# Silu gates by a hyperbolic tangent out of PSUM, and reciprocal square roots wholly on the vector engine, in the last two layers of a four-layer kernel

## The chip, the cores and the metric

The kernel runs on one core of a Trainium2 chip. The metric is the device time of one launch in microseconds (us), the median of several runs. The engines are named as in the profile: PE is the matrix engine (PEld its weight loads, which overlap it), DVE the vector engine, ACT the scalar engine, POOL the GpSimd engine, and SP the engine that issues most of the transfers.

## The reference, cut to what matters

Four layers work on 512 tokens of width 1024 in fp32. The change is in the last two: a differential attention and a neighbourhood attention, both over 512 tokens and a context of 256, both with an inner width of 2048, which the kernel splits into eight groups g.

```python
def diff_attention_mixer(u_lat, u_ctx, w_in, w_out, qn_g, kn_g, lam_vecs, subln_g, layer_idx, need_ctx):
    ...
        return (o.reshape(bsz, n, D_INNER) * jax.nn.silu(z)) @ w_out
...
def neighbourhood_mixer(u_lat, u_ctx, w_in, w_out, qn_g, kn_g, rpb, need_ctx):
    ...
    out_l = (o_l * jax.nn.silu(z_l)) @ w_out
...
def rms_norm(x, g):
```

In both, q and k are divided per head (64 wide) by their root mean square, the scores go through a softmax, and the output o of a head is multiplied by silu(z) = z / (1 + exp(-z)), where z is a projection of the layer's input. In the differential layer two softmaxes are subtracted, and o is divided by its own root mean square over 128 columns before the gate. So each layer needs, for every group, one set of gates and a few reciprocal square roots of small tiles (128 x 24, 128 x 16 or 128 x 6).

## The kernel before, in words

Each of the two layers is one loop over units that is written out by hand: in the differential layer (`diff_run`) a unit is (g, p, t), 12 to a group, 96 in all; in the neighbourhood layer (`na_run`) it is (g, h, j), 16 to a group, 128 in all. In every iteration the stages of neighbouring units stand in a fixed order in program text, and each engine takes its own instructions in that order: the scores of the new unit on PE (A), work that was put off by one iteration (`due`, which runs what `defer` took), one projection piece for the next group on PE, the minimum of the negated scores on DVE (B, L2116 and L2286), the transposes of the unit before on PE (T, L2152 and L2304), the exponentials on ACT (E), a second projection piece in some iterations, the value product on PE (G), and the scaling of the exponentials on DVE (Dm, L2138 to L2140 and L2296 to L2297). T of the next iteration waits for Dm. With t0 the first unit of a group, "t0+3" below is the fourth iteration of a group.

The projection pieces are 24 matmuls of 128x256 (a "mm" buffer in PSUM each) whose weights come as `w_raw` by SP, are rounded to `w_hi` by ACT (CAST, L276) and split into `w_lo` by POOL (L280). A piece of q or k leaves PSUM by ACT as `st` (a copy) and `sq` (its square), and DVE sums the square per head into `ssq` or `ssk` (L1777). When the last sum of a group is there, `finish` makes the reciprocal root by `rstd_parts`: L422 on DVE, a logarithm and an exponential on ACT, and one iteration later three operations of a Newton step on DVE (L432 to L434) and up to two scalings (L1792, L1795). `Hn` does the same for the 128 x 6 tile `oss` of a finished pair of heads, with its Newton step at L2180 to L2183; POOL then multiplies the output `ob` by the result (L2184). `H2` transposes `ob`, and DVE multiplies it by the gate (L2194).

A piece of z leaves PSUM by an ACT copy into `SZ`. `gates_at` sets out for every 128 columns of it an ACT exponential into `ge`, and an iteration later on DVE an addition (L1829) and a RECIPROCAL (L1830), and on POOL the product with z (L1831). In the neighbourhood layer the gate multiplies the output in POOL (L2331).

Of the kernel before, what the change touches and what calls it, by code (L numbers as in the profile page):

```python
# [380 lines left out]
class Net:  # L381
# [1254 lines left out]
    def tables2(s, pool, tmp):  # L1636
# [11 lines left out]
        def compute():  # L1648
# [26 lines left out]
    def second(s, L, nx):  # L1675
# [108 lines left out]
        def finish(n, g, k):  # L1784
            r = g2.tile([128, 24], F32, name=f"r{n}")
            rs = s.rstd_parts(r[:, :k], SS[n][:, :k], 1.0 / 64)
            next(rs)

            def two():
                next(rs, None)  # L1790
                if n == "q":
                    nc.vector.tensor_scalar(r[:, :k], r[:, :k], 0.125, None, OP.mult)  # L1792
                    if diff:
                        r2 = g2.tile([128, 24], F32, name="nrq")
                        nc.vector.tensor_scalar(r2, r, -1.0, None, OP.mult)  # L1795
                        scal[g] = r, r2
                        return
                for i in range(k // 4):
                    x = rawt[n][:, i].rearrange("p (h d) -> p h d", d=64)
                    nc.gpsimd.tensor_tensor(x, x, r[:, 4 * i:4 * i + 4].unsqueeze(2).to_broadcast([128, 4, 64]), OP.mult)  # L1800

            s.defer(two)

        def z_piece(g, b, t0):
            box = {}

            def mm():
                if t0 == 0:
                    hold("z", [f"z{L}:{g}:{b}"])
                box["ps"] = ps = s.mm.tile([128, 512], F32, name="mm")[:, :256]  # L1810
                for h in range(2):
                    s.fmm(ps, U["z"], uh, ul, t0, 256, ks=range(4 * h, 4 * h + 4))
                    yield

            return mm, lambda: s.act(SZ[g][b][:, t0:t0 + 256], box["ps"], AF.Copy)

        def gates_at(ts, g, chunks):

            e = {}

            def one(b, c):
                z = SZ[g][b][:, c * 128:(c + 1) * 128]
                e[b, c] = g2.tile([128, 128], F32, name="ge", bufs=3 if diff else 4)
                s.act(e[b, c], z, AF.Exp, scale=-1.0)

            def two(b, c):
                z = SZ[g][b][:, c * 128:(c + 1) * 128]
                x = e[b, c]
                nc.vector.tensor_scalar(x, x, 1.0, None, OP.add)  # L1829
                nc.vector.reciprocal(x, x)  # L1830
                nc.gpsimd.tensor_tensor(z, z, x, OP.mult)  # L1831

            for t, bc in sorted([(t + 1, (0, bc)) for t, bc in zip(ts, chunks)] + [(t, (1, bc)) for t, bc in zip(ts, chunks)]):
                put((early, extra)[bc[0]], t, lambda bc=bc: (two, one)[bc[0]](*bc[1]))

# [63 lines left out]
        def put(d, t, *x):  # L1899
            d.setdefault(t, []).extend(x)  # L1900

        ns = 12 if diff else 16
        for g in range(8):
# [3 lines left out]
            if diff and g < 7:  # L1907
# [4 lines left out]
                for j in range(6):  # L1912
                    put(fill, t0 + j, *qk[2 * j:2 * j + 2])
                at = (6, 6, 7, 8, 8, 9, 9, 10, 11, 12, 13, 14) if g < 6 else (6, 7, 7, 8, 8, 9, 13, 13, 14, 14, 15, 15)
                gates_at([t0 + t for t in at], g, [(b, c) for b in range(2) for c in range(6)])
                for t, f in zip((6, 7, 8, 9), stacks("q", 0) + stacks("k", 0)):
# [5 lines left out]
            elif diff:  # L1922
                for t, x in zip(Z7, zz):
                    put(fill, t0 + t, x)
                put(extra, t0 + 2, lambda: y_tile(), *[lambda b=b: y_dma(b) for b in range(5)])
                gates_at([t0 + t for t in (4, 5, 6, 7, 8, 9, 10, 11, 12, 13, 14, 15)], g, [(b, c) for b in range(2) for c in range(6)])
                put(extra, t0 + 5, lambda: y_dma(5))
                for b in range(8):
                    put(early, t0 + Y7[b], lambda b=b: y_split(b))
            else:  # L1930
                if g < 7:
                    vv = [piece("v", g + 1, i) for i in range(6)]
                    for t, x in zip((0, 1, 2, 3, 4, 5, 6, 7, 8, 9, 10, 11, 12, 13) + ((13, 14, 14, 15, 15, 16) if g < 6 else (14, 15, 15, 16, 16, 17)), qk + zz + vv):
# [143 lines left out]
    def diff_run(s, c):  # L2077
# [93 lines left out]
        def Hn(g, p):  # L2171
            o, ss, oe = O[g, p]
            v, y, a = [s.sml.tile([128, 6], F32, name=f"df_{k}") for k in "vya"]
# [12 lines left out]
            s.defer(two)  # L2186
# [45 lines left out]
    def na_run(s, c):  # L2232
# [158 lines left out]
```

## Time and profile before

| | |
|---|---|
| median of three runs | 3164.03 us (3159.46 to 3167.75) |
| profiled execution | 3165.68 us, span 3163.9 us, mean granted clock 0.990 |
| busy: PE, DVE, ACT, POOL | 3051.2, 1903.7, 1611.1, 1739.4 us |
| loop of the differential layer | about 1450 to 2260 us of the span, some 100 us a group |
| loop of the neighbourhood layer | about 2435 to 3060 us, some 83 us a group |

The times inside the kernel come from the profiled execution, whose time is 1.65 us over the median. PE is busy for 96 parts in a hundred of the span, so a change shows in the time where it makes PE wait, or stops a wait of PE.

### The profile page before, as it was taken

To read this page: it belongs to the slowest core of one execution; us is meant where nothing else is said; L and a number is where in the kernel's file an instruction comes from. 1 tells how busy PE (TensorE), PEld (TensorE's weight loads), DVE (VectorE), ACT (ScalarE), POOL (GpSimd) and SP (SyncE) were. 2 spreads that over 40 slices of the span, in tenths; PEclk is the share of its full clock that TensorE was granted. 3 is DMA by queue.
4 is the path that set the end of the run, shared out by engine and by line. 5 is a ranking of instruction groups with operands and counts; after the bars stand their busy time and mean duration, and the time that the engine had idled before them with its cause. 6 is when DMAs were issued, how large, how long until landed. Compare 5 with 4: busy or idle time off the path is not lost.

```text
span 3163.9 us, 59874 instructions
## 1 busy us (share of the span) xinstructions
PE 3051.2 (96%) x22868; PEld 2878.0 (91%) x22868; DVE 1903.7 (60%) x4163; ACT 1611.1 (51%) x3811; POOL 1739.4 (55%) x2390
## 2 busy tenths in 40 slices
PE   8999999998999999999999999998999999999989
PEld 7898889888899988899999999998999999999989
DVE  4875423345775333355777777677445777777764
ACT  4544533345775433345655555555325565656652
POOL 5543466664663656667556665563356545555545
PEclk9999999999999999999999999999999999999989
DMA  3122333434233434442222222213323233333334
GB/s 124 61 74 82 106 127 127 143 115 149 94 92 116 136 125 133 129 125 78 69 71 65 71 70 69 69 57 107 124 94 94 73 85 88 85 91 91 88 94 141
DMA packets 104555, 310.89 MB, mean 98 GB/s; under 512 B 19902, under 2 KB 33470, under 8 KB 100684
## 3 DMA queue, kind: packets, MB, share of 16 engines
q1 hardware_dynamic: 94908, 271.60, 26.3%
q0 software_dynamic: 7776, 31.46, 4.3%
q10 hardware_dynamic: 1584, 4.00, 0.4%
q8 instruction: 181, 2.97, 0.4%
q14 instruction: 106, 0.87, 0.1%
HBM read 258.73 MB, written 23.12 MB: 89 GB/s over the span
## 4 chain that ended last, share of the span: by engine, by line
PE 63%; DVE 4%; ACT 3%; DMA 2%; POOL 2%; issue 1%; SPq 0%; ACTq 0%; DVEq 0%; POOLq 0%
PE mm L587 16%; PE mm L589 16%; PE mm L588 16%; PE mm L2165 3%; PE tp L2304 2%; PE s L2105 1%; PE tp L2152 1%; DMA KL<-KL 1%; PE s L2106 1%; PE mm L2319 1%; PE mm L2314 1%; PE tp L1843 1%; PE s L2278 1%; ACT X L413 1%; POOL w_lo L280 1%
## 5 line engine op out<-in xcount | busy, mean ns | idle before, releaser
L280 POOL TENSOR_TENSOR w_lo<-w_raw,w_hi 128x256 fp32r<-128x256 f32 (+2 forms) x1438 | 1142.4, 826 | 804.2 <-ACT w_hi L276 771.1
L587 PE MATMUL mm<-w_hi,hh 128*128 128x256 f32 (+2 forms) x2752 | 801.9, 291 | 9.9 <-ACT w_hi L276 4.4
L588 PE MATMUL mm<-w_lo,hh 128*128 128x256 f32 (+2 forms) x2752 | 784.5, 285 | 5.8 <-POOL w_lo L280 3.9
L589 PE MATMUL mm<-w_hi,hl 128*128 128x256 f32 (+2 forms) x2752 | 783.5, 285 | 1.5 <-POOL hl L416 1.5
L587 PEld LDWEIGHTS mm<-w_hi,hh 128*128 128x128 f32 x2752 | 525.1, 191 | 20.0 <-ACT df_sq L413 6.3
L588 PEld LDWEIGHTS mm<-w_lo,hh 128*128 128x128 f32 x2752 | 525.7, 191 | 15.2 <-POOL w_lo L280 9.8
L589 PEld LDWEIGHTS mm<-w_hi,hl 128*128 128x128 f32 x2752 | 524.4, 191 | 3.0 <-POOL hl L416 2.2
L276 ACT CAST w_hi<-w_raw 128x1024 fp32r<-128x1024 f32 (+2 forms) x371 | 383.3, 1036 | 227.8 <-PE mm L589 186.2
L587 PE MATMUL mm<-hh,w_hi 128*128 128x256 f32 (+1 forms) x1408 | 454.8, 323 | 3.0 <-DVE M L1092 2.8
L588 PE MATMUL mm<-hl,w_hi 128*128 128x256 f32 (+1 forms) x1408 | 447.8, 318 | 0.6
L589 PE MATMUL mm<-hh,w_lo 128*128 128x256 f32 (+1 forms) x1408 | 446.5, 317 | 0.6 <-DVE w_lo L280 0.6
L587 PEld LDWEIGHTS mm<-hh,w_hi 128*128 128x128 f32 x1408 | 265.5, 189 | 30.9 <-issue 5.2
L587 PE MATMUL mm<-w_hi,gh 128*128 128x256 f32 x1024 | 287.8, 281 | 0.0
L589 PE MATMUL mm<-w_hi,gl 128*128 128x256 f32 x1024 | 287.2, 280 | 0.1
L588 PE MATMUL mm<-w_lo,gh 128*128 128x256 f32 x1024 | 287.0, 280 | 0.0
L588 PEld LDWEIGHTS mm<-hl,w_hi 128*128 128x128 f32 x1408 | 265.5, 189 | 22.3 <-DVE hl L347 1.8
L589 PEld LDWEIGHTS mm<-hh,w_lo 128*128 128x128 f32 x1408 | 265.1, 188 | 21.4 <-DVE w_lo L280 1.0
L416 DVE TENSOR_TENSOR gl<-rsq,gh 128x512 fp32r<-128x512 f32 x64 | 46.0, 719 | 269.1 <-ACT gh L413 269.1
L587 PEld LDWEIGHTS mm<-w_hi,gh 128*128 128x128 f32 x1024 | 193.2, 189 | 0.4
L589 PEld LDWEIGHTS mm<-w_hi,gl 128*128 128x128 f32 x1024 | 193.0, 188 | 0.5 <-DVE gl L416 0.5
L588 PEld LDWEIGHTS mm<-w_lo,gh 128*128 128x128 f32 x1024 | 193.0, 188 | 0.3
L413 ACT ACTIVATE wt<-tp 128x512 f32<-128x512 f32 (+1 forms) x96 | 50.5, 526 | 229.9 <-PE tp L2152 229.9
(385 smaller groups left out, 6963.5 us busy)
## 6 DMA issues: line engine op xcount, KB each, us to landing
w_raw<-in_w SPq DMA_DIRECT2D x352, 512.0 KB, 3.5
modw<-in_mod SPq DMA_DIRECT2D x24, 1024.0 KB, 5.9
KH<-KH POOLq DMA_DIRECT2D x32, 384.0 KB, 3.6
KL<-KL POOLq DMA_DIRECT2D x32, 384.0 KB, 4.9
xs<-X SPq DMA_DIRECT2D x12, 512.0 KB, 3.8
X<-xs SPq DMA_DIRECT2D x12, 512.0 KB, 7.1
yd<-ob SPq DMA_DIRECT2D x16, 384.0 KB, 2.4
w_raw<-in_w SPq DMA_DIRECT2D x8, 552.0 KB, 3.6
```

Of the source, the lines that this page charges most:

```text
L276: nc.scalar.copy(hi[:, :m], raw[:, :m])
L280: (eng or nc.gpsimd).tensor_tensor(lo[:, c], raw[:, c], hi.bitcast(F32)[:, c], OP.subtract)
L413: return s.nc.scalar.activation(out, in_, func, bias=bias, scale=scale, **kw)
L416: (eng or s.nc.vector).tensor_tensor(lo, x, hi.bitcast(F32), OP.subtract)
L587: mm(ps, ah, bh, start=first, stop=False)
L588: mm(ps, ah, bl, start=False, stop=False)
L589: mm(ps, al, bh, start=False, stop=last)
L1843: nc.tensor.transpose(pt[:, j], rawt[n][:, i, pr * 128:(pr + 1) * 128], s.ident)
L2105: nc.tensor.matmul(o, q, KH[:, h, a:b], start=True, stop=False)
L2106: nc.tensor.matmul(o, q, KL[:, h, a:b], start=False, stop=True)
L2165: nc.tensor.matmul(ps, x["w"][:, k], V[g][:, kb, p * 128:(p + 1) * 128], start=k == 0, stop=k == nk - 1)
L2304: nc.tensor.transpose(t[:, k], x["P"][:, k * 128:(k + 1) * 128], s.ident)
```

## The change

The gate is written as silu(z) = z/2 * (1 + tanh(z/2)). ACT reads the z piece in PSUM and writes tanh(z/2) for all 256 columns into `ge`, and one DVE operation, SCALAR_TENSOR_TENSOR, makes (ge + 1) * z out of `ge` and the same PSUM buffer straight into `SZ`; it runs at once in the differential layer and one iteration later in the neighbourhood layer. The factor of one half goes into `gs` and into the scaling of P in Dm. `gates_at` and its calls go. The reciprocal roots of these two layers are made by `rstd_root`: a guess of the square root from the bits of the number, two steps of Heron's rule, and a last reciprocal, 9 or 10 operations of DVE in one piece, at once in `finish`; in `Hn` 11 operations, all put off to the next iteration's `due`. No logarithm is left in the two layers, and the set of ACT's tables is changed by hand at their start and at the end of the first.

```diff
+    def rstd_root(s, r, ss, inv_n, c, eps=EPS):
+
+        n = r.shape[-1]
+        v = s.nc.vector
+        q, a = [s.small.tile([128, 24], F32, name=f"rr_{k}")[:, :n] for k in "qa"]
+        v.tensor_scalar(ss, ss, inv_n, eps, OP.mult, OP.add)
+        v.tensor_scalar(q.bitcast(I32), ss.bitcast(I32), 0.5, float(0x1FBB4F2E), OP.mult, OP.add)
+        v.reciprocal(a, q)
+        v.tensor_tensor(a, a, ss, OP.mult)
+        v.tensor_tensor(q, q, a, OP.add)
+        v.reciprocal(a, q)
+        v.tensor_tensor(a, a, ss, OP.mult)
+        v.scalar_tensor_tensor(q, q, 0.25, a, OP.mult, OP.add)
+        v.reciprocal(r, q)
+        if c != 1.0:
+            v.tensor_scalar(r, r, c, None, OP.mult)
...
-            nc.vector.tensor_scalar(gs, s.p("subln"), 1.0 - lam_init, None, OP.mult)
+            nc.vector.tensor_scalar(gs, s.p("subln"), 0.5 * (1.0 - lam_init), None, OP.mult)
...
-            r = g2.tile([128, 24], F32, name=f"r{n}")
-            rs = s.rstd_parts(r[:, :k], SS[n][:, :k], 1.0 / 64)
-            next(rs)
+            r = g2.tile([128, 24], F32, name=f"r{n}")[:, :k]
+            s.rstd_root(r, SS[n][:, :k], 1.0 / 64, 1.0 if n == "k" else -0.125 if diff else 0.125)
...
-            return mm, lambda: s.act(SZ[g][b][:, t0:t0 + 256], box["ps"], AF.Copy)
-
-        def gates_at(ts, g, chunks):
...
-                e[b, c] = g2.tile([128, 128], F32, name="ge", bufs=3 if diff else 4)
-                s.act(e[b, c], z, AF.Exp, scale=-1.0)
...
-                nc.vector.tensor_scalar(x, x, 1.0, None, OP.add)
-                nc.vector.reciprocal(x, x)
-                nc.gpsimd.tensor_tensor(z, z, x, OP.mult)
...
+            def ev():
+
+                ps, e = box["ps"], g2.tile([128, 256], F32, name="ge")
+                s.act(e, ps, AF.Tanh, scale=0.5)
+                mult = lambda: nc.vector.scalar_tensor_tensor(SZ[g][b][:, t0:t0 + 256], e, 1.0, ps, OP.add, OP.mult)
+                mult() if diff else s.defer(mult)
...
+        nc.scalar.preload_act_table_set(TANHEXP)
...
+        if diff:
+            nc.scalar.preload_act_table_set(LNEXP)
...
-            nc.vector.scalar_tensor_tensor(oe, oe, EPS, oe, OP.mult, OP.mult)
-            nc.vector.scalar_tensor_tensor(v, ss, 1.0 / 128, oe, OP.mult, OP.add)
-            s.act(y, v, AF.Ln)
-            s.act(y, y, AF.Exp, scale=-0.5)
+            y = s.sml.tile([128, 6], F32, name="df_y")
...
-                nc.vector.tensor_tensor(a, y, y, OP.mult)
-                nc.vector.tensor_tensor(a, a, v, OP.mult)
-                nc.vector.tensor_scalar(a, a, -0.5, 1.5, OP.mult, OP.add)
-                nc.vector.tensor_tensor(y, y, a, OP.mult)
+                nc.vector.scalar_tensor_tensor(oe, oe, 128 * EPS, oe, OP.mult, OP.mult)
+                nc.vector.tensor_tensor(ss, ss, oe, OP.add)
+                s.rstd_root(y, ss, 1.0 / 128, 1.0, 0.0)
...
-            nc.vector.tensor_scalar(x["P"], x["P"], r, None, OP.mult)
+            nc.vector.tensor_scalar(x["P"], x["P"], r, 0.5, OP.mult, OP.mult)
```

The order of instructions on DVE in a differential group, at t0+3 of `diff_run`, from Dm of one iteration to B of the next. Before:

```order
L2140 SCALAR_TENSOR_TENSOR X_66<-X_67,df_rb,X_66 128x768
L2174 SCALAR_TENSOR_TENSOR oe<-oe 128x6
L2175 SCALAR_TENSOR_TENSOR df_v<-oss,oe 128x6
L1777 TENSOR_REDUCE ssq<-sq 128x4 x2
L422 TENSOR_SCALAR rs_v<-ssq 128x24
L2180 TENSOR_TENSOR df_a<-df_y 128x6
L2181 TENSOR_TENSOR df_a<-df_a,df_v 128x6
L2182 TENSOR_SCALAR df_a<-df_a 128x6
L2183 TENSOR_TENSOR df_y<-df_y,df_a 128x6
L2116 ISA s_18167,df_nb<-s_18167,zero,nrq 128x768
```

After, where L446 to L456 are the lines of `rstd_root` and L2114 is B:

```order
L2138 SCALAR_TENSOR_TENSOR X_66<-X_67,df_rb,X_66 128x768
L1795 TENSOR_REDUCE ssq<-sq 128x4 x2
L446 TENSOR_SCALAR ssq<-ssq 128x24
L447 TENSOR_SCALAR rr_q<-ssq 128x24
L448 RECIPROCAL rr_a<-rr_q 128x24
...
L456 TENSOR_SCALAR rq<-rq 128x24
L2174 SCALAR_TENSOR_TENSOR oe<-oe 128x6
L2175 TENSOR_TENSOR oss<-oss,oe 128x6
L446 TENSOR_SCALAR oss<-oss 128x6
...
L454 RECIPROCAL df_y<-rr_q 128x6
L2114 ISA s_18124,df_nb<-s_18124,zero,rq 128x768
```

Between the last sum of squares and B there stood five operations; now there are the ten of the root for q and the eleven of `Hn`.

The same engine in a neighbourhood group, at t0+10 of `na_run`, where the last sum of squares of k comes. Before:

```order
L1777 TENSOR_REDUCE ssk<-X_69 128x4
L422 TENSOR_SCALAR rs_v<-ssk 128x24
L2286 ISA s_29822,na_nb<-s_29822,bm_29265 128x512
L2286 ISA na_nb 128x1
L416 TENSOR_TENSOR ptl<-tp,pth 128x512
L2296 RECIPROCAL na_r<-na_s 128x1
L2297 TENSOR_SCALAR X_66<-X_66,na_r 128x512
L432 TENSOR_TENSOR rs_a<-rs_y 128x24
```

After, where L2279 is B and L2290 the scaling in Dm:

```order
L1795 TENSOR_REDUCE ssk<-X_69 128x4
L446 TENSOR_SCALAR ssk<-ssk 128x24
L447 TENSOR_SCALAR rr_q<-ssk 128x24
L448 RECIPROCAL rr_a<-rr_q 128x24
L449 TENSOR_TENSOR rr_a<-rr_a,ssk 128x24
...
L454 RECIPROCAL rk<-rr_q 128x24
L2279 ISA s_29511,na_nb<-s_29511,bm_28952 128x512
L2279 ISA na_nb 128x1
L417 TENSOR_TENSOR ptl<-tp,pth 128x512
L2289 RECIPROCAL na_r<-na_s 128x1
L2290 TENSOR_SCALAR X_66<-X_66,na_r 128x512
```

One operation stood ahead of B there, and now nine do.

Later in the same group, at t0+13, where gates were made. Before:

```order
L2286 ISA s_30122,na_nb<-s_30122,bm_29266 128x512
L416 TENSOR_TENSOR ptl<-tp,pth 128x512
L1829 TENSOR_SCALAR ge<-ge 128x128
L1830 RECIPROCAL ge<-ge 128x128
...
L2296 RECIPROCAL na_r<-na_s 128x1
L2297 TENSOR_SCALAR X_66<-X_66,na_r 128x512
```

After:

```order
L1831 SCALAR_TENSOR_TENSOR SZ<-ge,mm 128x256
...
L2279 ISA s_29811,na_nb<-s_29811,bm_28953 128x512
L2279 ISA na_nb 128x1
L417 TENSOR_TENSOR ptl<-tp,pth 128x512
L2289 RECIPROCAL na_r<-na_s 128x1
L2290 TENSOR_SCALAR X_66<-X_66,na_r 128x512
```

The two pairs L1829 and L1830 ahead of Dm are gone there, and the new operation of the gate stands ahead of an earlier B.

## Rows read from the trace of the kernel before

**Rows 1.** The page, part 1: busy time, share of the span, instructions.
```profile
PE 3051.2 (96%) x22868; PEld 2878.0 (91%) x22868; DVE 1903.7 (60%) x4163; ACT 1611.1 (51%) x3811; POOL 1739.4 (55%) x2390
```
**Rows 2.** A window of 100 us: busy of PE, PEld, DVE, ACT, POOL; clock; DMA.
```profile
1750.00:1850.00 100.00, 98.30 (x808) 96.13 (x808) 73.72 (x170) 57.15 (x173) 60.61 (x92) 1.00 0.23 69
```
**Rows 3.** Waits of PE, 1450 to 2100 us: total, times, longest.
```profile
PE tp L1843 <- DVE ob L2194: 8.5, 6, 1.4
...
PE mm L587 <- ACT df_sq L413: 0.9, 6, 0.2
```
**Rows 4.** Waits of PE, 2100 to 2290 us.
```profile
PE s L2105 <- ACT X L413: 5.1, 6, 1.4
PE tp L2152 <- DVE X L2140: 5.0, 2, 4.7
```
**Rows 5.** Waits of PE, 2460 to 3000 us.
```profile
PE tp L2304 <- DVE X L2297: 7.3, 12, 2.0
PE s L2278 <- DMA KL<-KL: 2.1, 6, 0.7
```
**Rows 6.** Waits of PE, 3000 to 3164 us.
```profile
PE tp L2304 <- DVE X L2297: 5.3, 3, 4.4
PE s L2277 <- DMA KH<-KH: 2.3, 1, 2.3
```
**Rows 7.** A window at the last group change, same columns.
```profile
2990.00:3020.00 30.00, 24.39 (x175) 23.55 (x175) 20.98 (x46) 14.44 (x39) 10.14 (x19) 0.89 0.33 88
```
**Rows 8.** Groups of instructions: count, busy us, mean ns, idle before.
```profile
L1830 DVE RECIPROCAL ge<-ge 128x128 f32<-128x128 f32 x160 | 152.5, 953 | 5.5
...
L413 ACT ACTIVATE X<-s,na_nb 128x512 f32<-128x512 f32 x128 | 87.7, 685 | 30.5 <-DVE na_nb L2286 30.1
...
L2296 DVE RECIPROCAL na_r<-na_s 128x1 f32<-128x1 f32 x128 | 18.4, 144 | 3.9 <-ACT X L413 3.8
```
**Rows 9.** Timeline of DVE at 1579, ahead of B.
```profile
1578.64 0.42 DVE L1777 TENSOR_REDUCE ssq<-sq 128x4 f32<-128x256 f32 x1 [0.43 <-ACT sq L413]
...
1579.18 0.16 DVE L2180 TENSOR_TENSOR df_a<-df_y 128x6 f32<-128x6 f32 x1
1579.38 0.17 DVE L2181 TENSOR_TENSOR df_a<-df_a,df_v 128x6 f32<-128x6 f32 x1
...
1579.86 1.02 DVE L2116 CUSTOM_DVE_ANT_0 s<-s,zero,nrq 128x768 f32<-128x768 f32 x1
```
**Rows 10.** Timeline of ACT at 1583 to 1587.
```profile
1583.21 0.92 ACT L413 ACTIVATE X<-s,df_nb 128x768 f32<-128x768 f32 x1
...
1584.96 1.07 ACT L276 CAST w_hi<-w_raw 128x1024 fp32r<-128x1024 f32 x1
1586.58 0.28 ACT L413 ACTIVATE ob<-mm 128x128 f32<-128x128 f32 x1 [0.55 <-PE mm L2165]
```
**Rows 11.** Timeline of PE at 1587.
```profile
1587.16 0.39 PE L587 MATMUL mm<-w_hi,hh 128*128 128x256 f32 x1
```
**Rows 12.** Timeline of DVE at 2561 to 2563: B and the scaling in Dm.
```profile
2561.40 0.69 DVE L2286 CUSTOM_DVE_ANT_0 s<-s,bm 128x512 f32<-128x512 f32 x1
...
2563.26 0.49 DVE L2297 TENSOR_SCALAR X<-X,na_r 128x512 f32<-128x512 f32 x1
```
**Rows 13.** Timeline of PE at 2564.7: the transposes of T.
```profile
2564.70 0.60 PE L2304 MATMUL tp<-ident,X 128*128 128x128 f32 x4
```
**Rows 14.** Timeline of ACT at 54: a load of tables and the next operation.
```profile
54.23 1.28 ACT L413 ACT_TABLE_LOAD   x1
55.52 0.21 ACT L413 ACTIVATE cg<-par 128x16 f32<-128x16 f32 x1
```
**Rows 15.** Timeline of all engines at 1586, two rows of POOL and DVE.
```profile
1585.89 1.37 POOL L1773 TENSOR_TENSOR st<-X,X 128x256 f32<-128x256 f32 x1
...
1586.58 0.73 DVE L432 TENSOR_TENSOR rs_a<-rs_y 128x24 f32<-128x24 f32 x1
```
**Rows 16.** Waits of PE, 1389 to 1450 us: the differential layer's start.
```profile
PE mm L587 <- ACT sq L413: 1.8, 1, 1.8
```

More of the change, by code (lines that the diff above doesn't have):

```diff
@@ L30 @@
 LNEXP = "natural_log_exp_and_others"
+TANHEXP = "exp_and_others"
 def plan():
@@ L1784, in finish @@
         def finish(n, g, k):
-            r = g2.tile([128, 24], F32, name=f"r{n}")
-            rs = s.rstd_parts(r[:, :k], SS[n][:, :k], 1.0 / 64)
-            next(rs)
+            r = g2.tile([128, 24], F32, name=f"r{n}")[:, :k]
+            s.rstd_root(r, SS[n][:, :k], 1.0 / 64, 1.0 if n == "k" else -0.125 if diff else 0.125)
             def two():
[L1790 to L1797, printed above, removed]
+                if n == "q" and diff:
+                    scal[g] = r
+                    return
                 for i in range(k // 4):
@@ L1813, in mm @@
                     yield
-            return mm, lambda: s.act(SZ[g][b][:, t0:t0 + 256], box["ps"], AF.Copy)
-        def gates_at(ts, g, chunks):
-            e = {}
-            def one(b, c):
-                z = SZ[g][b][:, c * 128:(c + 1) * 128]
-                e[b, c] = g2.tile([128, 128], F32, name="ge", bufs=3 if diff else 4)
-                s.act(e[b, c], z, AF.Exp, scale=-1.0)
-            def two(b, c):
-                z = SZ[g][b][:, c * 128:(c + 1) * 128]
-                x = e[b, c]
-                nc.vector.tensor_scalar(x, x, 1.0, None, OP.add)
-                nc.vector.reciprocal(x, x)
-                nc.gpsimd.tensor_tensor(z, z, x, OP.mult)
-            for t, bc in sorted([(t + 1, (0, bc)) for t, bc in zip(ts, chunks)] + [(t, (1, bc)) for t, bc in zip(ts, chunks)]):
-                put((early, extra)[bc[0]], t, lambda bc=bc: (two, one)[bc[0]](*bc[1]))
+            def ev():
[3 more added lines that the diff above has]
+                mult() if diff else s.defer(mult)
+            return mm, ev
         def stack(n, pr, tiles):
@@ L1913, in second @@
                     put(fill, t0 + j, *qk[2 * j:2 * j + 2])
-                at = (6, 6, 7, 8, 8, 9, 9, 10, 11, 12, 13, 14) if g < 6 else (6, 7, 7, 8, 8, 9, 13, 13, 14, 14, 15, 15)
-                gates_at([t0 + t for t in at], g, [(b, c) for b in range(2) for c in range(6)])
                 for t, f in zip((6, 7, 8, 9), stacks("q", 0) + stacks("k", 0)):
@@ L1925, in second @@
                 put(extra, t0 + 2, lambda: y_tile(), *[lambda b=b: y_dma(b) for b in range(5)])
-                gates_at([t0 + t for t in (4, 5, 6, 7, 8, 9, 10, 11, 12, 13, 14, 15)], g, [(b, c) for b in range(2) for c in range(6)])
                 put(extra, t0 + 5, lambda: y_dma(5))
@@ L1934, in second @@
                         put(fill, t0 + t, x)
-                    gates_at([t0 + t for t in (12, 13, 13, 14, 14, 15, 15, 16)], g, [(b, c) for b in range(2) for c in range(4)])
                     for t, f in zip((12, 13, 14), stacks("q", 0) + stacks("k", 0)):
@@ L1945, in second @@
                         put(fill, t0 + t, x)
-                    gates_at([t0 + t for t in (7, 8, 9, 10, 11, 12, 13, 14)], g, [(b, c) for b in range(2) for c in range(4)])
                     put(extra, t0 + 2, *[lambda b=b: y_dma(b) for b in range(6)])
@@ L2110, in B @@
             x = d[u]
-            nrq = c.scal[g][1]
+            nrq = c.scal[g]
             for j in range(2):
@@ L2172, in Hn @@
             o, ss, oe = O[g, p]
-            v, y, a = [s.sml.tile([128, 6], F32, name=f"df_{k}") for k in "vya"]
-            nc.vector.scalar_tensor_tensor(oe, oe, EPS, oe, OP.mult, OP.mult)
-            nc.vector.scalar_tensor_tensor(v, ss, 1.0 / 128, oe, OP.mult, OP.add)
-            s.act(y, v, AF.Ln)
-            s.act(y, y, AF.Exp, scale=-0.5)
+            y = s.sml.tile([128, 6], F32, name="df_y")
             def two():
-                nc.vector.tensor_tensor(a, y, y, OP.mult)
-                nc.vector.tensor_tensor(a, a, v, OP.mult)
-                nc.vector.tensor_scalar(a, a, -0.5, 1.5, OP.mult, OP.add)
-                nc.vector.tensor_tensor(y, y, a, OP.mult)
+                nc.vector.scalar_tensor_tensor(oe, oe, 128 * EPS, oe, OP.mult, OP.mult)
+                nc.vector.tensor_tensor(ss, ss, oe, OP.add)
+                s.rstd_root(y, ss, 1.0 / 128, 1.0, 0.0)
                 nc.gpsimd.tensor_tensor(o, o, y.unsqueeze(2).to_broadcast([128, 6, 128]), OP.mult)
```

## The prediction

> **What bounds the kernel now.** I read the busy shares first: PE is busy 3051.2 of 3163.9 us [rows 1], so no other engine's work is worth its length; only waits of PE count, and those are 3163.9 - 3051.2 = 112.7 us in the whole kernel, most of them outside these two layers. Second, the windows: in 100 us of the differential loop PE is busy 98.30, at full clock, with DVE at 73.72, ACT at 57.15 and POOL at 60.61 [rows 2]. Third, the waits of PE, stage by stage. In the differential loop the only wait that repeats with weight is that of the transposes of q and k pieces for the gate's product `ob`, 8.5 us over 6 groups [rows 3]; that product follows the transposes of `H2`, which stand behind a Dm, not behind a gate. In the tail of that loop PE waits 5.1 us for the exponentials and 5.0 for Dm [rows 4]. In the neighbourhood loop it waits 7.3 us at T for Dm, in 12 pieces, the longest 2.0, and 2.1 us for the transfer of KL [rows 5]; in the last group 5.3 us at T and 2.3 for KH [rows 6]. Around the last group change the granted clock is 0.89 [rows 7], a part of the window at the lower of the two levels, after PE had idled.
>
> **What the change removes.** On DVE 160 reciprocals of 953 ns go, 152.5 us [rows 8], with the additions ahead of them; on POOL the 160 products; on ACT two small operations for each root and 160 exponentials, while the tanh takes the place of the copy out of PSUM. In the differential loop that is nearly all work beside a busy PE and worth nothing by itself. It is worth something where a gate stands ahead of what PE waits for:
>
> The neighbourhood loop, at t0+12 to t0+15. In the order before, one or two gates stand between `ptl` and Dm; the reciprocal alone is 0.95 us [rows 8]. After, none do. So I take the waits at T there as gone, without the longest: 7.3 - 2.0 = 5.3, and the waits for KL with them, 2.1, since POOL and ACT reach that transfer earlier: a gain of 7.4 us. Bounds: 3 (T's alone, in part) and 9.4 (all of it).
>
> The last group change and the last group, 2.0 + 5.3 = 7.3 us of waits at T. Here a transfer of KH is right behind (2.3 us) [rows 6], whose wait grows when PE comes to it earlier, so I take 3 of 7.3. Bounds: 0 and 7.3, and above that what the clock gives back: at 0.89 of 30 us [rows 7] that is 3.3 us.
>
> The tail of the differential loop: of 10.1 us [rows 4] most is ACT's own pace and I take 2. Bounds: 0 and 10.1.
>
> Gains together: 7.4 + 3 + 2 = 12.4 us.
>
> **What it adds.** *The price of a chain.* Small operations of DVE start 0.20 us apart [rows 9]. A reciprocal takes 144 ns on one column and 953 on 128 [rows 8], 6.4 ns a column, so I estimate 0.29 us on 24 columns and 0.18 on 6, with 0.04 between. The root of q has 7 other operations and 3 reciprocals: 7 x 0.20 + 3 x 0.33 = 2.4 us; that of k has one operation less, 2.2; that of `Hn` 8 x 0.20 + 3 x 0.22 = 2.3.
>
> *Differential loop, t0+3.* The sums end at 1578.64 + 0.42 = 1579.06 and B starts at 1579.86 [rows 9]. With both chains ahead of it (the first two order listings) B starts at 1579.06 + 2.4 + 2.3 = 1583.8, that is 3.9 us later. The first exponential started at 1583.21 [rows 10], though B's first minimum was there at 1579.86 + 1.02 = 1580.9; so 2.3 us are slack and the exponentials come 1.6 late. Queued behind them on ACT is the rounding of weights, which ended at 1584.96 + 1.07 = 1586.03, and then the copy of the value product, `ob`, at 1586.58: slack again 0.55, so this copy is 1.05 us late. The first matmul of the next piece, at 1587.16 [rows 11], takes that buffer and waits for it already (for `df_sq`) [rows 3]. A loss of 1.05 us in each of 7 groups: 7.4 us. Bounds: at operations of 0.16 us, their bare length [rows 9], the two slacks hide it, 0; if POOL stands in the way, below.
>
> *Differential loop, t0+6 and t0+8.* At t0+6 the chain of k, 2.2 us, takes the place of one operation ahead of B; a slack of 2.3 like the one at t0+3 hides it, and at t0+8 the eleven operations of `Hn` replace four and a turn through ACT. I take 0; without that cover the first costs up to 2.0 in 6 groups, 12 us.
>
> *Neighbourhood loop, t0+10.* Nine operations instead of one ahead of B (the third and fourth order listings): B comes 2.2 - 0.2 = 2.0 us later than at 2561.40 [rows 12]. The exponential waits for nothing but B (30.1 of 30.5 us of its idle time) [rows 8], so Dm ends at 2563.26 + 0.49 + 2.0 = 2565.75. T started at 2564.70 [rows 13], so PE waits 1.05 us; in 7 groups 7.4 us. Bounds: 0.5 a group at bare lengths (3.5), 2 if the slack is gone. The chain of q, five iterations before, has a value product ahead of the next T and I take it as covered.
>
> *The tables.* A load of ACT's tables takes 1.28 us, and the next operation starts 1.29 after it did [rows 14]. Three are added. The one at the differential layer's start stands ahead of the pieces' first copies, where PE waits for ACT already (1.8 us) [rows 16]; so does that at the next layer's start; the third is followed by transfers and I take it as hidden: 2 x 1.3 = 2.6 us. Bounds: 0 and 3.9. The Trainium skill, "ScalarE: Activation LUTs", section "What ACT_TABLE_LOAD costs", puts a change of tables at about 2.66 us, a load of 1283 ns and a drain of some 1380. The load agrees with the row; no drain shows there, and by the page's figure the two would be 5.3 us, 2.7 more than in the sum.
>
> *The gate's own operation.* 80 of them, in place of two reciprocals each; behind Dm in the differential layer and one iteration late in the other; nothing is due behind them that PE waits for. 0.
>
> **The sum.** 7.4 + 7.4 + 2.6 - 12.4 = +5.0 us on the profiled 3165.7, so 3170.7; the median is 1.65 lower, so 3169 us. That is 0.16% over before: no change that this measurement can tell (0.3%, 9.5 us).
>
> **The rivals.**
> *The chains are hidden, and what went pays* (faster). Both losses rest on slacks read in one group each, 2.3 and 0.95 us, while ACT and DVE lose work ahead of these places. If half a microsecond more of slack stands at each, the losses fall to about 7, and if all of it is hidden there remain 2.6 - 12.4 = -9.8, with the clock 3.3 more: 3151 to 3156. It decides from chains under 2.7 us for both at t0+3 (less than 0.13 an operation) or E's turn coming later anyway. Against it: the order of B is fixed behind the chains.
>
> *The chains meet POOL* (slower). The Newton operation at 1586.58 took 0.73 us and ended with a POOL operation that had begun at 1585.89 and lasted 1.37 [rows 15], where others take 0.16 [rows 9]. If the 6 or 7 operations of a chain that are not reciprocals each take 0.5 longer, a chain of q or k costs 3 us more; if half of the 14 chains in the two loops are hit, 7 x 3 = 21 us: 3190. For it: POOL is busy 60 of 100 us [rows 2]. Against it: at t0+3 and t0+10 the operations around B ran at 0.16 to 0.20, and POOL waits there for the chain's own result. The Trainium skill, "SBUF — State Buffer", section "Who interferes with whom", says the same as a rule: an operation of DVE with two inputs in SBUF, or one in a mode with two ports, waits out an operation of GpSimd that reads SBUF. The row agrees; by this rule the four operations of each root with two tensors are the exposed ones.
>
> *The loads of tables and the last transfers.* If nothing is gained at the last group change (KH is waited for instead) and the tables cost 5, the time is 3175: just over the bound.
>
> **How the numbers follow.** The forecast has 0.52; its own range is 3160 to 3178, of which 0.38 lies within 0.3%, 0.12 above and 0.02 below. The first rival has 0.27 (0.25 faster, 0.02 same), the second and third 0.21, slower. So faster 0.27, same 0.40, slower 0.33. The range reaches into both rivals: down to 3148 (most of the hidden chains with the clock), up to 3190 (half of the chains hit).
>
> **What would show it.** In the waits of PE of the changed kernel: T's waits in the neighbourhood loop no longer at t0+13 and t0+14 but one a group at t0+10, of about 1 us; a wait of the first matmul of a piece for `df_sq` of about 1.3 us a group in place of 0.15; the rows of `ob` as before. In DVE's timeline at t0+3: 21 operations over 4.7 us, reciprocals at 0.29 and 0.18. Three table loads of 1.28 us. The prediction is wrong if the chains take under 3 us or over 7 at t0+3, if exponentials of the differential layer are not queued ahead of the copy of `ob`, or if the clock's dips come or go elsewhere.

## The result

The changed kernel takes 3183.59 us (median of five runs, 3181.22 to 3187.63) against 3160.77 of before in the same five rounds (3159.46 to 3167.75): a ratio of 1.0067, 95% interval 1.0056 to 1.0077. It is slower by some 21 us. The forecast was 3169, no change, with 0.33 for slower; the time lies inside the range of 3148 to 3190, on the slow side of it.

The page of the changed kernel, part 1, as in [rows 1]:

```profile
PE 3051.1 (96%) x22868; PEld 2877.3 (90%) x22868; DVE 1785.8 (56%) x4155; ACT 1568.6 (49%) x3558; POOL 1651.9 (52%) x2230
```

PE does the same work in the same 22868 matmuls, while DVE does 118 us less, ACT 43 and POOL 87. The kernel is slower all the same. The profiled execution took 3181.51 us, 15.8 more than the profiled one of before, whose 3165.68 was 4.9 above its own median of five; so the traces show 15.8 of the 21 us, and the rest is the spread of single executions. A part of that spread is the clock's: the profiled execution of before was granted 0.990, while 34 of the 44 executions of before beside the experiments were granted 0.991 or 0.992, and 0.001 of the clock is up to 3.2 us of such a span. The profiled execution of the changed kernel was granted 0.990 too, so the 15.8 us as a whole are not the clock's, though single stages are in part, as said below.

Since PE runs the same matmuls in the same order in every kernel of this study but for its waits, the k-th matmul of one trace can be set against the k-th of another: the difference of their starts says how far a kernel is behind, and the growth of that difference says where it fell behind. The table gives this growth by stages of before's time, in us, and the last column the whole of it. Every entry is two starts from PE's timelines, subtracted.

| kernel | to 1390 | first start, to 1480 | differential loop, to 2110 | its tail, to 2400 | second start, to 2470 | neighbourhood loop, to 2990 | rest | all |
|---|---|---|---|---|---|---|---|---|
| changed | 1.7 | 3.3 | 9.6 | -0.5 | 3.8 | 1.9 | -4.1 | 15.9 |
| e1_roots | 1.9 | -0.4 | 8.4 | 3.5 | 2.8 | 8.8 | -0.1 | 24.9 |
| e2_noroot | 2.4 | 3.3 | 0.1 | -1.8 | -2.6 | -6.5 | -4.3 | -9.3 |
| e3_late | 0.8 | 5.1 | 7.7 | -1.0 | 4.2 | 3.8 | -5.4 | 15.2 |
| e4_tab | 1.1 | -0.3 | 9.8 | -1.2 | 4.6 | 2.3 | -3.2 | 13.2 |
| e5_start | 0.2 | -0.5 | 9.9 | -1.8 | -1.3 | 2.3 | -4.6 | 4.1 |
| e6_place | 1.3 | 5.1 | 0.3 | -0.3 | 2.5 | -6.8 | -4.0 | -2.0 |
| e7_all | 1.3 | -0.4 | 0.3 | -3.0 | 0.6 | -6.2 | -4.2 | -11.6 |
| e8_hn | 5.2 | 1.3 | 34.0 | 3.4 | 0.5 | 2.2 | -2.7 | 44.1 |
| e9_dose | 2.6 | 3.3 | 24.0 | 1.8 | 4.2 | 2.0 | -3.5 | 34.5 |
| e10_block | 0.2 | 4.7 | 9.5 | 4.8 | 4.0 | 2.1 | -3.9 | 21.4 |

Nothing was changed before 1390 us, so the first column, 0.2 to 5.2, is how far two executions differ by themselves; it is the measure for what a single entry can say.

**The profile after.** Waits of PE from 1450 to 2100 us (total, times, longest), against [rows 3]:

```profile
PE tp L1843 <- DVE ob L2187: 8.5, 6, 1.4
PE mm L605 <- ACT df_sq L414: 6.9, 12, 1.1
PE mm L2163 <- DVE SZ L1831: 1.9, 6, 0.4
```

The wait for `ob` is the same 8.5 us to the tenth. That for `df_sq` went from 0.9 to 6.9, and one for the gate's new operation (SZ, 1.9) is new. DVE's timeline at t0+3, against [rows 9]: the last sum, the first operation of q's root and a reciprocal of it, a reciprocal of the pair's root, and B.

```profile
1584.48 0.42 DVE L1795 TENSOR_REDUCE ssq<-sq 128x4 f32<-128x256 f32 x1 [0.78 <-ACT sq L414]
1584.93 0.18 DVE L446 TENSOR_SCALAR ssq<-ssq 128x24 f32<-128x24 f32 x1
...
1585.36 0.30 DVE L448 RECIPROCAL rr_a<-rr_q 128x24 f32<-128x24 f32 x1
...
1588.13 0.19 DVE L448 RECIPROCAL rr_a<-rr_q 128x6 f32<-128x6 f32 x1
...
1589.49 0.99 DVE L2114 CUSTOM_DVE_ANT_0 s<-s,zero,rq 128x768 f32<-128x768 f32 x1
```

Twenty-one operations take 1589.49 - 1584.93 = 4.6 us. The first matmul of the next piece, the one of [rows 11], in PE's timeline:

```profile
1593.93 0.38 PE L605 MATMUL mm<-w_hi,hh 128*128 128x256 f32 x1 [1.12 <-ACT df_sq L414]
```

It waits 1.12 us for the release by `df_sq`. Set against its time in the trace of before it fell back by 0.97 us at this instruction.

The neighbourhood loop, against [rows 5]:

```profile
PE tp L2297 <- DVE X L2290: 8.8, 13, 1.1
PE s L2271 <- DMA KL<-KL: 1.2, 2, 1.0
```

The sum at T is 8.8 us for 7.3, of which 2.0 had been the last group change, but its places are others: T at t0+10, the one of [rows 13], now waits, as PE's timeline shows,

```profile
2583.86 0.63 PE L2297 MATMUL tp<-ident,X 128*128 128x128 f32 x4 [1.05 <-DVE X L2290]
```

and those behind the gates are 0.2 us or nothing in most groups, where they had been 0.3 to 0.6. A loss of 1.2 us a group at the one place, and gains of 0.4 to 0.8 and of 0.3 at the two others and of 0.3 to 0.4 at the transfer of KL in most groups (the growth of the difference at these matmuls), nearly cancel; the loop ends 1.9 us further behind.

### The profile page after: what moved, and what is told of

Its sections match the earlier page's. It is cut to its first block, busy times and chain, and to the rows that moved or that the text cites. A ratio compares the mean times of both kernels' runs of the same rounds, so it can differ in the third digit from the quotient of the medians.

```text
span 3179.7 us, 59513 instructions
## 1 busy us (share of the span) xinstructions
PE 3051.1 (96%) x22868; PEld 2877.3 (90%) x22868; DVE 1785.8 (56%) x4155; ACT 1568.6 (49%) x3558; POOL 1651.9 (52%) x2230
## 4 chain that ended last, share of the span: by engine, by line
PE 58%; DVE 7%; ACT 5%; issue 2%; POOL 2%; DMA 1%; SPq 0%; DVEq 0%; ACTq 0%; POOLq 0%
PE mm L605 15%; PE mm L607 14%; PE mm L606 14%; PE mm L2163 2%; ACT X L414 2%; PE tp L2297 1%; PE tp L2150 1%; PE s L2103 1%; PE s L2104 1%; PE tp L1843 1%; PE mm L2312 1%; PE mm L2307 1%; DMA KL<-KL 1%; PE s L2271 1%; PE mm L787 1%
## 5 line engine op out<-in xcount | busy, mean ns | idle before, releaser
L281 POOL TENSOR_TENSOR w_lo<-w_raw,w_hi 128x256 fp32r<-128x256 f32 (+2 forms) x1438 | 1140.6, 825 | 912.7 <-ACT w_hi L277 879.7
L607 PEld LDWEIGHTS mm<-hh,w_lo 128*128 128x128 f32 x1408 | 265.0, 188 | 21.4 <-DVE w_lo L281 1.0
```

What stands on the lines that cost most here:

```text
L281: (eng or nc.gpsimd).tensor_tensor(lo[:, c], raw[:, c], hi.bitcast(F32)[:, c], OP.subtract)
L607: mm(ps, al, bh, start=False, stop=last)
```

## The experiments

Each ratio is against runs of before on the same chip; e1 to e4 shared them, e5 to e7, and e8 and e9.

**e1_roots.** The roots alone, put into the kernel of before; gates by exponential and reciprocal.

```diff
+    def rstd_root(s, r, ss, inv_n, c, eps=EPS):
...
-            rs = s.rstd_parts(r[:, :k], SS[n][:, :k], 1.0 / 64)
-            next(rs)
+            s.rstd_root(r, SS[n][:, :k], 1.0 / 64, 1.0 if n == "k" else -0.125 if diff else 0.125)
...
-            s.act(y, v, AF.Ln)
-            s.act(y, y, AF.Exp, scale=-0.5)
...
+                s.rstd_root(y, ss, 1.0 / 128, 1.0, 0.0)
```

> Only the reciprocal roots are made by the vector engine's chains; the gates stay as they were before (exponential, addition, reciprocal, product), and no tables are changed. Theory (the chains that stand ahead of B are the loss): PE waits 1.0 us more for df_sq at t0+3 in 7 differential groups, 1.2 us more at T at t0+10 in 7 neighbourhood groups, with nothing given back by the gates: 15 us over before, about 3176 us. Rival (the gate's new operation, which holds a PSUM buffer until the vector engine has read it, is the loss): within 3 us of before, 3158 to 3164.

Measured: 3191.48 us, ratio 1.0082 (1.0068 to 1.0096). The roots alone lose 27 us, more than the whole change. The differential loop loses 8.4 us and the neighbourhood loop 8.8, with nothing given back; the start of the neighbourhood layer loses 2.8 though no table is loaded there. That was not expected.

**e2_noroot.** The gates alone: of each root one reciprocal is left.

```diff
     def rstd_root(s, r, ss, inv_n, c, eps=EPS):
...
+        s.nc.vector.reciprocal(r, ss)
```

> The changed kernel with each chain of nine or ten operations replaced by one reciprocal, so the roots are left out of the computation; gates and table loads as changed. Theory: what is left is the gain of the gates in the neighbourhood loop (7 us) and its tail (3), against the table loads (3 to 6) and 0.5 us a group for the buffer that the gate holds: 1 to 6 us under before, about 3157. Rival (the gate is the loss): 10 to 20 us over before.

Measured: 3154.24 us, ratio 0.9965 (0.9951 to 0.9979). The waits of PE from 2480 to 3010 us:

```profile
PE tp L2283 <- DVE X L2276: 1.6, 6, 0.5
```

T's waits fell to 1.6 us in all. The gates are a gain of 11 us even with the loads of tables, and the new operation costs the differential loop nothing (0.1). The rival that the gate is the loss is gone. The first start still loses 3.3 us here, so that is not the roots'.

**e3_late.** All chains behind Dm.

```diff
-                    finish(n, g, 4 * seen[n, g])
...
+                        s.late.append(lambda: finish(n, g, k))
...
             for _, ev in pcs[1:]:
                 ev()
+            for f in s.late:
+                f()
+            s.late = []
...
         def Hn(g, p):
...
+            nc.vector.scalar_tensor_tensor(oe, oe, 128 * EPS, oe, OP.mult, OP.mult)
+            nc.vector.tensor_tensor(ss, ss, oe, OP.add)
+            s.rstd_root(y, ss, 1.0 / 128, 1.0, 0.0)
...
             def two():
-                nc.vector.scalar_tensor_tensor(oe, oe, 128 * EPS, oe, OP.mult, OP.mult)
-                nc.vector.tensor_tensor(ss, ss, oe, OP.add)
-                s.rstd_root(y, ss, 1.0 / 128, 1.0, 0.0)
```

> The changed kernel with the chains moved behind Dm of their iteration (the one of a finished pair not put off any more), the same operations. Theory: the wait for df_sq falls back to 0.15 us a group and that at t0+10 of the neighbourhood loop to under 0.6: 10 to 14 us under the changed kernel, about 3171. Rival (it is the amount of work on the vector engine, not its place): no change from 3183.

Measured: 3184.68 us, ratio 1.0061 (1.0048 to 1.0074): no gain, and the rival seemed right. The waits of PE from 1450 to 2100 us say why it is not:

```profile
PE tp L2158 <- DVE QS L417: 6.3, 6, 1.1
PE mm L607 <- ACT df_sq L414: 1.9, 12, 0.2
```

The wait for `df_sq` fell to 1.9 us in 12 as the theory had it, but the root of k, now behind Dm at t0+6, stands ahead of the split of QS, and PE waits for that 1.1 us a group instead. In the neighbourhood loop the wait moved by one iteration in the same way. The place behind Dm was good for q and bad for k.

**e4_tab.** The loads of tables moved.

```diff
-        nc.scalar.preload_act_table_set(TANHEXP)
+        put(extra, 1, lambda: nc.scalar.preload_act_table_set(TANHEXP))
+        if diff:
+            put(extra, 93, lambda: nc.scalar.preload_act_table_set(LNEXP))
```

> The changed kernel with its three loads of tables moved from the layers' starts and end into the loops (iterations 1 and 93 of the differential, 1 of the neighbourhood layer). Theory: the 1.4 us at the first start and some 1 to 3 at the second come back: 3 to 5 us under the changed kernel, about 3179. Rival (a load costs the same wherever it stands, by a drain of ACT): no change or slower.

Measured: 3180.97 us, ratio 1.0047 (1.0034 to 1.0060), about 6 us under the changed kernel's ratio. The first start is mended whole (-0.3 for 3.3). The second is not (4.6).

**e5_start.** As e4, and the roots of the first group of each layer by logarithm and exponential as before.

```diff
-            s.rstd_root(r, SS[n][:, :k], 1.0 / 64, 1.0 if n == "k" else -0.125 if diff else 0.125)
+            if g == 0:
+                rs = s.rstd_parts(r, SS[n][:, :k], 1.0 / 64)
+                next(rs)
+            else:
+                s.rstd_root(r, SS[n][:, :k], 1.0 / 64, c)
...
```

> The changed kernel with only its starts mended: the first group's roots of each layer by logarithm and exponential as before, and the loads of tables moved into the loops. Theory (the two starts cost 3.5 and some 5 us, the first by the load of tables, the second by the chains ahead of the first KH and KL transfers): 8 us under the changed kernel, that is 13 over before. Rival (the second start lost by the load and the clock): only the 4 to 5 us that moving the loads alone gave back.

Measured: 3173.51 us, ratio 1.0027 (1.0016 to 1.0038): 8.5 over before, where 13 was expected. Both starts are back at before's or better (-0.5 and -1.3). At the second it was the chains, in which alone e5 differs from e4: there the product with the root, the transposes and the transfers of KH and KL follow each other, and PE waits for KL. The waits, in e4, e5 and before:

```profile
PE s L2271 <- DMA KL<-KL: 3.4, 1, 3.4
PE s L2280 <- DMA KL<-KL: 2.2, 1, 2.2
...
PE s L2278 <- DMA KL<-KL: 2.0, 1, 2.0
```

The wait is not the whole of the 5.9 us between e4 and e5. The windows with it, in e4, e5 and before (columns as in [rows 2]), show that the clock differs as well, 0.83 in e4 and 1.00 in e5, which is up to 0.17 x 20 = 3.4 us of PE's work:

```profile
2440.00:2460.00 20.00, 16.16 (x110) 15.58 (x109) 7.82 (x23) 7.61 (x15) 6.70 (x11) 0.83 0.58 121
2440.00:2460.00 20.00, 18.00 (x147) 17.74 (x148) 12.45 (x39) 10.90 (x24) 6.56 (x9) 1.00 0.37 93
...
2420.00:2440.00 20.00, 18.03 (x139) 17.74 (x138) 10.88 (x25) 9.28 (x19) 9.69 (x17) 0.91 0.65 148
```

**e6_place.** The chains in other places, starts as changed: in the differential loop k's root between B and Dm, q's and the pair's behind Dm; in the neighbourhood loop two halves behind Dm of two iterations.

```diff
+            for f in s.mid:
+                f()
+            s.mid = []
             for f in c.early.get(i, []):
                 f()
             if u[2]:
                 G(u[2])
             if u[0]:
                 Dm(u[0])
...
```

> The changed kernel with its chains in other places of the same iterations: the root of k in the differential loop between B and Dm, where the vector engine waits for the exponentials, that of q and the one of a finished pair behind Dm; in the neighbourhood loop in two halves behind Dm of two iterations. Starts and tables as changed. Theory (the place of a chain sets its price): the differential loop loses nothing a group, the neighbourhood loop gains its 1 us a group, so 16 us under the changed kernel, within 8 over before. Rival (the work itself delays what follows wherever it stands): 5 us or less under the changed kernel.

Measured: 3163.77 us, ratio 1.0000 (0.9991 to 1.0009), 21 us under the changed kernel's ratio with the same operations. The waits, 1450 to 2100 and 2480 to 3000 us:

```profile
PE mm L613 <- ACT df_sq L414: 2.0, 13, 0.2
...
PE tp L2323 <- DVE X L2316: 1.6, 6, 0.5
```

The differential loop loses 0.3 us in six groups and the neighbourhood loop gains 6.8. The new wait for SZ is gone without a change of the gate.

**e7_all.** e5 and e6 together; in `finish`, which begins the chain as a generator of two halves:

```diff
+            root = s.rstd_steps(r, SS[n][:, :k], 1.0 / 64, c) if g else s.rstd_parts(r, SS[n][:, :k], 1.0 / 64)
...
```

> Both together: chains in the other places, first roots as before, loads of tables in the loops. Theory: nothing is left of the losses, and the gates' removal pays in the neighbourhood loop and the tails: 8 to 12 us under before, a ratio of 0.9965. Rival: about before.

Measured: 3155.06 us, ratio 0.9973 (0.9962 to 0.9984): faster than before by 8 to 10 us (5 to 12 by the interval), and 9.4 parts in a thousand faster than the changed kernel by their ratios. It is the fastest of the kernels that leave nothing out.

**e8_hn.** The pair's chain alone moved behind Dm at t0+2; the edit is that of `Hn` in e3.

```diff
+            s.rstd_root(y, ss, 1.0 / 128, 1.0, 0.0)
...
-                s.rstd_root(y, ss, 1.0 / 128, 1.0, 0.0)
```

> The changed kernel with one thing moved: the eleven operations of a finished pair run behind Dm at once and are not put off to stand ahead of B with the ten of q. Theory (at t0+3 one chain of 2.4 us lies inside a slack of 2.3, two of 4.7 do not): the wait for df_sq of 1.1 us a group falls to the 0.15 of before though the root of q still stands ahead of B, 1.0 us a group in 7 groups, 6 to 7 us under the changed kernel, with the differential loop at 0.5 to 0.6 us a group over before (the root of k and the buffer that the gate holds). Rival (the root of q alone, or the place of its last sums, makes the wait): half of it or less comes back.

Measured: 3209.47 us, ratio 1.0143 (1.0129 to 1.0157): 24 us over the changed kernel by their ratios, where 7 under was expected. The expectation was wrong twice. It forgot that the two sums of squares stand behind the moved chain, so that less of it leaves the way to B than its length. And POOL and DVE met, as all engines' timeline shows at t0+3:

```profile
1587.65 1.47 POOL L2177 TENSOR_TENSOR ob<-ob,df_y 128x768 f32<-128x768 f32 x1 [1.16 <-DVE df_y L454]
...
1588.22 0.93 DVE L446 TENSOR_SCALAR ssq<-ssq 128x24 f32<-128x24 f32 x1
...
1589.08 2.82 POOL L281 TENSOR_TENSOR w_lo<-w_raw,w_hi 128x256 fp32r<-128x256 f32 x4
...
1589.19 0.66 DVE L447 TENSOR_SCALAR rr_q<-ssq 128x24 int32<-128x24 int32 x1
...
1589.88 0.30 DVE L448 RECIPROCAL rr_a<-rr_q 128x24 f32<-128x24 f32 x1
...
1590.58 0.66 DVE L450 TENSOR_TENSOR rr_q<-rr_q,rr_a 128x24 f32<-128x24 f32 x1
...
1593.38 1.01 DVE L2114 CUSTOM_DVE_ANT_0 s<-s,zero,rq 128x768 f32<-128x768 f32 x1
```

With the pair's root ready at 1587.6, POOL multiplied `ob` and went on with the split of weights (L281), while q's root ran: 0.93 and 0.66 us for operations of 0.18, the reciprocal at its 0.30, and the chain took 1593.46 - 1588.22 = 5.2 us instead of 2.4. PE falls back by 1.9 us at the scores and 1.4 at the piece, in place of 0.97 in all. The clock adds to it: in windows of 25 us from t0+3 on it is 0.93 in five of the six groups and 0.86 in one, where the changed kernel has 1.00, so up to 0.07 x 25 = 1.8 us of PE's work go in a group. The first of them, in e8 and in the changed kernel:

```profile
1580.00:1605.00 25.00, 21.74 (x168) 21.17 (x167) 15.80 (x44) 11.99 (x33) 14.54 (x21) 0.93 0.27 72
...
1580.00:1605.00 25.00, 23.73 (x198) 23.14 (x197) 14.90 (x50) 11.96 (x36) 16.43 (x24) 1.00 0.21 59
```

**e9_dose.** Five more operations behind q's root at t0+3.

```diff
+            if diff and n == "q" and g:
+                for _ in range(5):
+                    nc.vector.tensor_scalar(r, r, 1.0, None, OP.mult)
```

> The changed kernel with five more operations of 0.2 us behind the root of q in the differential loop, which multiply by one. Theory (the slack is spent, so each further microsecond ahead of B at t0+3 is one of PE's): 1.0 us more in each of 7 groups, 7 us over the changed kernel, seen at the first matmul of the piece after t0+3. Rival (the wait is set by something else that the chain only uncovers): under 2 us more.

Measured: 3197.84 us, ratio 1.0103 (1.0089 to 1.0118). At t0+3 PE now falls back by 2.0 us (0.58 at the scores and 1.43 at the piece) in place of 0.97, in six groups: a microsecond for a microsecond. But the loop lost 24.0 in place of 9.6, twice the dose of 7. Windows of 25 us from t0+3, of two groups (busy of PE, PEld, DVE, ACT, POOL, then the granted clock):

```profile
1580.00:1605.00 25.00, 23.09 (x192) 22.52 (x191) 16.29 (x54) 11.98 (x33) 13.94 (x20) 1.00 0.22 54
...
1690.00:1715.00 25.00, 22.94 (x176) 22.16 (x175) 15.44 (x53) 10.15 (x31) 17.08 (x26) 0.93 0.14 43
```

In every second group the clock falls behind the stall: 0.93 of a window means a piece of it at 1.2 GHz in place of 2.4, and PE loses some 1.5 us more there (the difference grows by 3.6 us around these groups, by 2.0 around the others).

**e10_block.** As e8, but the last reciprocal of the pair's root stays put off, behind q's root.

```diff
+            nc.vector.tensor_copy(yq, h)
...
             def two():
...
+                nc.vector.reciprocal(y, yq)
                 nc.gpsimd.tensor_tensor(o, o, y.unsqueeze(2).to_broadcast([128, 6, 128]), OP.mult)
```

> As the run before with the pair's chain behind Dm, but its last reciprocal is still put off and stands behind the root of q (with a copy of six columns more), so that GpSimd's product of ob, and the splitting of weights queued behind it, wait for the root of q again. Theory (there the chain of q met GpSimd, since GpSimd was set free too early): the operations of q take 0.2 us again in place of 0.65, B starts some 5.8 us behind Dm's end in place of 8.6, the differential loop costs 1 to 1.6 us a group over before in place of 5.6, and the time is that of the changed kernel or a few us less. Rival (the chain at this place delays the sums and B by itself): 4 us a group or more, 3200 us.

Measured: 3188.15 us, ratio 1.0078 (1.0062 to 1.0095), 21 us under e8. DVE's timeline at t0+3:

```profile
1587.00 0.18 DVE L447 TENSOR_SCALAR rr_q<-ssq 128x24 int32<-128x24 int32 x1
...
1587.77 0.18 DVE L450 TENSOR_TENSOR rr_q<-rr_q,rr_a 128x24 f32<-128x24 f32 x1
...
1589.28 0.98 DVE L2116 CUSTOM_DVE_ANT_0 s<-s,zero,rq 128x768 f32<-128x768 f32 x1
```

The operations of q are at 0.18 us again and PE falls back by 0.71 at the piece. Ten operations and a copy of the chain stand where they stood in e8; only POOL is held back. So it was POOL that the chain met in e8; and with the smaller loss the clock stays at 1.00 in that loop. The tail of the differential layer lost 4.8 us here and 3.4 in e8, which was not followed up.

## Why the prediction was right in places and wrong in the sum

**The price of a chain: right.** The reciprocals take 0.30 us on 24 columns and 0.19 on 6 (0.29 and 0.18 forecast), both chains at t0+3 4.6 us (4.7). The limit that was set for the first rival, 2.7 us for both, leaves out the 0.80 us that lay between the sums and B before: with the two slacks it is 0.80 + 2.3 + 0.55 = 3.65 us. The 4.6 us are over either.

**Differential loop, t0+3: right.** B starts 3.8 us later behind the last sum (3.9), and 0.97 us were lost at the very matmul that was named (1.05), for `df_sq`, in six groups, and 0.23 in the first; e9 shows the slack spent and e6 the loss gone with the chains.

**Differential loop, t0+6: the cover failed.** It was set at 0. Here the rival that was named came in: k's root met POOL's split of weights, as the timeline of all engines shows:

```profile
1612.10 2.82 POOL L281 TENSOR_TENSOR w_lo<-w_raw,w_hi 128x256 fp32r<-128x256 f32 x4 [0.46 <-PE s L2104]
1612.34 0.53 DVE L446 TENSOR_SCALAR ssk<-ssk 128x24 f32<-128x24 f32 x1
1612.90 0.66 DVE L447 TENSOR_SCALAR rr_q<-ssk 128x24 int32<-128x24 int32 x1
...
1614.31 0.66 DVE L450 TENSOR_TENSOR rr_q<-rr_q,rr_a 128x24 f32<-128x24 f32 x1
...
1615.33 0.18 DVE L452 TENSOR_TENSOR rr_a<-rr_a,ssk 128x24 f32<-128x24 f32 x1
...
1615.99 0.94 DVE L2114 CUSTOM_DVE_ANT_0 s<-s,zero,rq 128x768 f32<-128x768 f32 x1
...
1617.78 0.42 DVE L1831 SCALAR_TENSOR_TENSOR SZ<-ge,mm 128x256 f32<-128x256 f32 x1
```

From 1612.34 to B at 1615.99 are 3.65 us in place of 2.2: up to the end of the split at 1614.92 operations of 0.18 us take 0.33 to 0.66, and behind it 0.18 again. The gate's operation stands behind B, so at 1617.78 it still holds the PSUM buffer that the value product wants: 0.5 us a group, the wait for SZ. By itself the gate's operation costs nothing (e2). With a root of 2.2 us it would come 1.45 us earlier, which is more than this wait of at most 0.4; that is worked out, and no run shows POOL's share here alone. With the old gate the root of k loses 0.36 us a group just behind this place, for `df_sq` (e1). At t0+8, set at 0 too, nothing was lost. So the loop lost 9.6 us where 7.4 were forecast.

The Trainium skill, "SBUF — State Buffer", section "Who interferes with whom", says that an operation of DVE with two inputs in SBUF contends with one of GpSimd that reads SBUF, that one with a single input does so only in a mode with two ports, and that operations of one tensor and constants can enter such a mode. The rows of e8 agree: the operations with two tensors and those with one tensor and constants took 0.66 to 0.93 us, the reciprocal its 0.30.

**Neighbourhood loop, t0+10: right.** 1.2 us a group (1.05). **The gates' gain there: right.** The changed loop fell back by 1.9, that with the roots alone by 8.8: 6.9 us from the gates, 7.4 forecast. From 2990 us on the changed kernel gained 4.1 (3 forecast), and by the way that was named: the 2.2 us won at T at the group change went back at the transfer of KH, which is waited for 5.0 us in place of 2.3 [rows 6], and the last group gave the rest. In the tail of the differential loop it gained 0.5 (2 forecast), and that is no proof of the mechanism: the wait for the exponentials grew from 5.1 [rows 4] to 7.0 us, while the mean clock from there to the layer's end was 0.98 for 0.97 before, up to 2.9 us in 290. The two waits:

```profile
PE s L2270 <- DMA KH<-KH: 5.0, 1, 5.0
PE s L2103 <- ACT X L414: 7.0, 7, 2.1
```

**The tables: the term that was mis-sized.** 2.6 us were set for both starts; they lost 3.3 and 3.8. At the first the load took its 1.28 us and PE fell back by 1.5 at the first piece behind it, where it waits for `sq` 3.2 us in place of 1.8 [rows 16]; the rest is the clock. That wait, ACT's timeline at the load, and two windows around the start, after and before (columns as in [rows 2]):

```profile
PE mm L605 <- ACT sq L414: 3.2, 1, 3.2
```
```profile
1408.05 1.28 ACT L1950 ACT_TABLE_LOAD   x1
1409.34 0.38 ACT L414 ACTIVATE st<-mm 128x256 f32<-128x256 f32 x1
```
```profile
1400.00:1420.00 20.00, 16.76 (x121) 16.56 (x120) 11.59 (x28) 9.57 (x22) 11.22 (x19) 0.83 0.35 107
...
1440.00:1460.00 20.00, 15.96 (x111) 14.16 (x110) 15.46 (x29) 11.19 (x22) 14.01 (x22) 0.92 0.61 162
```
```profile
1400.00:1420.00 20.00, 18.21 (x142) 18.01 (x141) 14.10 (x30) 9.32 (x25) 13.50 (x23) 0.91 0.33 106
...
1440.00:1460.00 20.00, 15.61 (x118) 13.99 (x117) 12.15 (x21) 10.08 (x22) 12.40 (x21) 1.00 0.62 167
```

In these two windows before had 0.91 and 1.00; after has 0.83 and 0.92, a longer piece at 1.2 GHz in the one and a new one in the other, up to 0.08 x 20 = 1.6 us of lost work each, where PE did not wait anyway. The other kernels with the load in this place bear that out. From 1380 to 1480 us the mean clock is 0.97 in before and in e8, 0.93 in the changed kernel, e2 and e9, and 0.91 in e3, e6 and e10; the first start lost 1.3 in e8, 3.3 in the next three and 4.7 to 5.1 in the last. So the load itself cost the 1.3 us that were set for it, and what the forecast left out is the clock. The next operation starts 1.29 us after the load; as in [rows 14], no drain shows. At the second start the load was not the loss at all (e4 leaves 4.6, e1 has 2.8 without it): it was the chains ahead of the first transfers, which the prediction did not price, and with them the clock: 0.83 in a window of 20 us as in e4, for 0.91 before, up to 1.6 of the 3.8 us. In e8, where the clock stayed at 1.00 there, the same chains and load lost 0.5. The prediction looked for chains in the loops and not in the lead-in, where PE waits for the transfer of KL.

**The sum.** +5.0 us was forecast and the traces show +15.9: of the 10.9 missing 4.5 are the two starts, 2.2 the differential loop, 1.5 its tail, 1.9 the neighbourhood loop, 1.7 lies ahead of all that was changed, and the rest gained 1.1 more than forecast (rounded). The rival that the chains are hidden is refuted (e9). That they meet POOL holds at t0+6, and at t0+3 only where POOL is set free early (e8, e10). Behind these, some 5 us between the traces' difference and that of the medians stay unplaced, but for the part that is the clock's.

## What to carry to other kernels

An operation that costs nothing on an idle engine has a price by its place in that engine's order: the same chains cost 21 us more ahead of what PE waits for than in the holes between, where the two loops lost nothing by them (e6). Look for these places in the lead-in too, where PE waits for the first transfers, and put what is loaded once, like tables, where the engine waits anyway. Where operations of two engines hold each other up, as those of DVE and POOL did here, an operation that holds the one back can be what keeps the other fast (e8, e10), so moving it must be priced on both. Price a wait of PE together with the clock that follows it: in the loops of e8 and e9 and at both starts of the changed kernel the clock cost, on top of the wait, more than half of what the wait did.

## What the runs showed of the hardware

A stall of PE of 1 us a group left the clock at 1.00 (the changed kernel); with 2.0 us it fell in every second group, and each fall cost 1.5 us more (e9); with 3.4 us it fell in each of six groups (e8). This is what the runs show of it and no rule. The first load of tables cost 1.3 to 5.1 us for its 1.28, by the clock that came with it (0.97 to 0.91 over 100 us). An operation of DVE that changes 24 columns took up to 0.93 us beside a product of POOL over 768 columns, against 0.18 alone.
